# FFN 1's second product in six groups: where the norm vector is scaled, where m4 units are prepared, and when the casting transfers are issued

## The chip, the cores and the metric

The kernel runs on 1 core of one Trainium2 chip. The metric is the device time of one execution in microseconds (us), lower is better. The kernel before takes 1105.27 us, the median of 3 runs (1104.59 to 1105.53).

The engines are named as the profile names them: PE is TensorE (PEld its weight loads), DVE is VectorE, ACT is ScalarE, POOL is GpSimd and SP is SyncE. Each engine works through its own instructions in the order in which the program writes them. SP and POOL also issue DMA transfers, each in its own order.

## The reference

One layer of a hybrid encoder: 512 tokens, 1024 channels, float32. FFN 1, the mixer (a gated linear recurrence and a windowed attention side by side) and FFN 2 follow each other, each with a norm before and after it:

```python
f = swiglu(rms_norm(h, ffn1_pre_g[l]), ffn1_w1[l], ffn1_w3[l], ffn1_w2[l])
h = h + 0.5 * rms_norm(f, ffn1_post_g[l])
u = rms_norm(h, mix_pre_g[l])
q, k, v, xr, xg = jnp.split(u @ w_in[l], splits, axis=-1)
...
def swiglu(x, w1, w3, w2):
    return (jax.nn.silu(x @ w1) * (x @ w3)) @ w2
```

The change concerns the place where the product with `w2` of FFN 1 ends, the two norms behind it are taken (`ffn1_post_g`, then `mix_pre_g`), and the product with `xr` begins. The inner width of the FFN is 2816, that is 22 blocks of 128.

## The kernel before, in words

**Exactness.** Every operand of a product is split in two parts, a rounded one (`hi`) and the remainder (`lo`), and each product is three matmuls (hi x hi, lo x hi, hi x lo). `split2` (L224) is one split: ACT copies to `hi` (L226), DVE subtracts (L227). There are two ways to make `lo` without DVE: ACT copies the negated `hi`, and a DMA transfer that POOL issues adds the source on top. `cast_split` (L168) does so for weights in `BY_CAST`, whose `hi` is written by a transfer that rounds on the way (L147), and `prep` does so for the units in `BY_ADD` (L706 to L709).

**The product with w2 (class `Halves`, L600).** It is done with seven half-sized products instead of eight, in the order m1, m5, m2, m6, m3, m7, m4. Each of the seven goes over G = 6 groups of `w2` blocks (`GS_A`; five groups of two blocks, the last of one), so there are 42 units: 0 to 5 are m1, 24 to 29 m3, 30 to 35 m7, 36 to 41 m4. A unit is 12 matmuls of 128x512, two blocks by two token tiles by three (6 for the last of each six). `prep(n)` (L685) makes the operands of all units below n ready: two weight tiles (`whi`, `wlo`; one in a last unit) and the activations (`uT`, for the units from 36 on a tile `hx` of their own). `step(u)` (L753) calls `prep(u + LEAD)` with `LEAD = 5`, then the unit's hooks, then writes its matmuls. m7 and m4 add up in the same two banks, one for each token tile; between them DVE reads the bank (`out`, L744), so unit 36 has to wait for that.

**The buffers.** All large tiles come from one pool of 42 buffers (`NSLOT`) of 4 KB a partition. A tile that is first written takes the buffer that has been free longest in the order of the program, and its first writer waits until the earlier tile's last readers are done. So a tile that is asked for earlier shifts which buffers the tiles after it get.

**The end of the product (`tok_gemm` with `pre`, L434 to L482).** Steps 0 to 29 are written first, with hooks: after unit 18's preparation the two norm vectors are fetched by POOL (L294), after unit 22's step number ACT scales the second one by a constant (L438, in the order of ACT behind the preparation of unit 26), and at the numbers in `X_AT` = 26, 28, 31, 33 the four casting transfers of `xr` blocks 0 to 3 are issued by POOL. Then `prep(38)` readies units 34 to 37, and norm 0 follows: the norms of token tile 0 (`norms`, L326, with `post_norm`, L297). In the middle of it, behind the row factor (L277) and ahead of the addition to `h` (L322), it calls a function `mid`; before, that is `x_split(0)`, one ACT copy and a POOL transfer. Then units 38 and 39 are readied, `x_split(1)` follows, and steps 30 to 33; units 34 and 35 are written per token tile, with DVE's reading of the bank (L744) behind each, and with the preparation of unit 40 behind the first and unit 41 behind the second. Norm 1 follows with `x_split(2)` as its `mid`, then m4's units for tile 0, the transposes of the normed rows, and so on to norm 3 and the first matmuls with `xr`.

**Line numbers of what the steps touch:** casting transfer L147; negated copy and accumulating transfer of `xr` L172, L174; ACT and DVE part of a split L226, L227; scaling L438; negated copy and transfer in `prep` L707 to L709; matmuls of the units L732 to L734; reading of the bank L744; norm 0: L308 (adding the parts), L310 (squares), L311, L322 (`h`), L334 (squares of `h`), L337, L345 and L346 (normed row); transposes L355.

Of the kernel before, what the change touches and what calls it, by code (L numbers as in the profile page):

```python
# [12 lines left out]
AF = mybir.ActivationFunctionType  # L13
# [38 lines left out]
def hybrid_layer(ctx: ExitStack, tc: tile.TileContext, a: dict, out: bass.AP):  # L52
    nc = tc.nc
    act, dve, pool, pe, sp = nc.scalar, nc.vector, nc.gpsimd, nc.tensor, nc.sync
# [16 lines left out]
    def small(w, name="m", bufs=4):  # L71
        uid[0] += 1
        return sm.tile([P, w], F32, tag=f"sm{w}", name=f"{name}_{uid[0]}", bufs={1: 11, 4: 12}.get(w, bufs))
# [79 lines left out]
    def dma_to(n):  # L153
        while st["dma"] < min(n, len(order)):
            dma_one(st["dma"])
            st["dma"] += 1
# [11 lines left out]
    def cast_split(k):  # L168
        assert k == st["split"]
        dma_to(k + 1)  # L170
        pairs[k] = hi, lo = raws.pop(k), slot([P, D], F32R, name="wlo")
        act.activation(lo, f32(hi), AF.Copy, scale=-1.0)  # L172
        nm, i = order[k]
        pool.dma_start(out=lo, in_=a[nm][i * P : (i + 1) * P, :], accum_op=ALU.add)  # L174
        st["split"] += 1

    def split_to(n):
        while st["split"] < min(n, len(order)) and st["split"] not in paired:
            k = st["split"]
            dma_to(k + 1)  # L180
            r = raws.pop(k)
            if order[k] in BY_DMA:
                nm, i = order[k]
                pairs[k] = split_dma(r, a[nm][i * P : (i + 1) * P, :])
            else:
                hi = slot([P, D], F32R, name="whi")
                lo = slot([P, D], F32R, name="wlo")
                if order[k] in BY_POOL:
                    pool.tensor_copy(hi, r)
                else:  # L190
                    act.activation(hi, r, AF.Copy)
                dve.tensor_tensor(out=lo, in0=r, in1=f32(hi), op=ALU.subtract)
                pairs[k] = (hi, lo)
            st["split"] += 1
# [66 lines left out]
    NEWT = -0.5 * D**0.5  # L261
# [64 lines left out]
    def norms(acc, t, gpost, scale, gpre, spill, eps, mid=None, part=None, ns=(0, 1)):  # L326

        hg = slot([P, D], name="hg")
        junk = slot([P, D], name="junk")
        ss = small(2, "ss")  # L330
        rs = Rstd2()

        def half(n, c):
            act.activation(junk[:, c], h[t][:, c], AF.Square, accum_out=ss[:, n : n + 1])  # L334
            if n:
                rs.first(ss)
                dve.tensor_tensor(out=hg[:, c], in0=h[t][:, c], in1=gpre[:, c], op=ALU.mult)  # L337

        post_norm(acc, t, gpost, scale * NEWT, h[t], half, eps=eps, mid=mid, part=part, ns=ns)
        ht = h[t]  # L340
        if spill:
            sp.dma_start(out=h_scr[t], in_=h.pop(t))
        rs.root(ss)
        r = rs.value()
        dve.scalar_tensor_tensor(out=hg[:, :512], in0=ht[:, :512], scalar=r, in1=gpre[:, :512], op0=ALU.mult, op1=ALU.mult)  # L345
        act.activation(hg[:, 512:], hg[:, 512:], AF.Copy, scale=r)  # L346
        return hg

    def transpose_mm(hg):
        banks = []  # L350
        for half in range(2):
            ps = bank("tr")
            for k in range(4):
                kk = half * 4 + k
                pe.transpose(ps[:, k * P : (k + 1) * P], hg[:, kk * P : (kk + 1) * P], ident)  # L355
            banks.append(ps)
        return banks

    def transpose_out(banks, t, xf=None, parts=(0, 1)):
        c = slice(t * P, (t + 1) * P)  # L360
        for half, ps in enumerate(banks):
            ks = slice(half * 4, half * 4 + 4)
            v = ps.rearrange("p (k c) -> p k c", k=4)
            if 0 in parts:
                act.activation(uT[:, 0, ks, c], v, AF.Copy)
            if 1 in parts:
                dve.tensor_tensor(out=uT[:, 1, ks, c], in0=v, in1=f32(uT[:, 0, ks, c]), op=ALU.subtract)
        if xf:
            transpose_xf(banks, t, xf)

    def transpose_xf(banks, t, xf, halves=(0, 1)):
        for half in halves:
            ps = banks[half]
            v = ps.rearrange("p (k c) -> p k c", k=4)
            act.activation(xf[half, t // 2][:, :, (t % 2) * P : (t % 2 + 1) * P], v, AF.Copy)


    def tok_gemm(nm, xs, n, R, gpost_name, scale, gpre_name, first, x_to=None, xf=None, spill=False, then=None, eps=None, pre=None):
# [34 lines left out]
        g, us, trs = [], {}, {}  # L413
        ep = lambda t: D * EPS if eps is None else eps[:, t : t + 1]

        def vectors():
            g.extend((bcast(gpost_name), bcast(gpre_name)))
            if not pre:
                pool.tensor_scalar(out=g[1], in0=g[1], scalar1=NEWT, scalar2=None, op0=ALU.mult)

        def tails():
            for i, k in enumerate(tail):
                x_to(F + i + 1)
                w[k] = get(nm, k, ahead=max(0, len(tail) - 1 - i), rawahead=0 if pre else 2)
# [6 lines left out]
        def norm(t, mid=None):  # L431
            us[t] = norms(acc[t], t, g[0], scale, g[1], spill, ep(t), mid, pre and pre.part(t), (1, 0) if pre and t > 1 else (0, 1))

        if pre:  # L434
            G = pre.G
            pre.hooks[3 * G].append(vectors)
            pre.hooks[3 * G + 1].append(lambda: act.activation(small(1, "tiny"), veps[:, 0:1], AF.Abs_reciprocal_sqrt))
            pre.hooks[3 * G + 4].append(lambda: act.activation(g[1], g[1], AF.Copy, scale=NEWT))  # L438
            x0 = st["get"] + len(tail)
            for i, u in enumerate(X_AT):  # L440
                pre.hooks[u].append(lambda i=i: dma_to(x0 + i + 1))

            def x_split(i):
                cast_split(x0 + i)

            for u in range(5 * G):
                pre.step(u)
            for t in range(2):
                acc[t] = [pre.bank["bc"][t], pre.bank["bx"][t]]
            pre.prep(5 * G + LEAD + 3)  # L450
            norm(0, lambda: x_split(0))
            pre.prep(7 * G - 2)
            x_split(1)
            for u in range(5 * G, 6 * G - 2):
                pre.step(u)
            for t in range(2):
                for u in range(6 * G - 2, 6 * G):
                    pre.step(u, (t,))
                pre.prep(7 * G - 1 + t)
            for t in range(2, 4):  # L460
                acc[t] = [pre.bank["bu"][t - 2], None]
            pre.hid.eo.clear()
            norm(1, lambda: x_split(2))
            for u in range(6 * G, 7 * G):
                pre.step(u, (0,))
            trs[0] = transpose_mm(us[0])
            transpose_out(trs[0], 0)
            for u in range(6 * G, 6 * G + 2):
                pre.step(u, (1,))
            trs[1] = transpose_mm(us[1])  # L470
            transpose_out(trs[1], 1)
            x_split(3)
            norm(2, lambda: [transpose_xf(trs[0], 0, xf), transpose_xf(trs[1], 1, xf, (0,))])
            transpose_xf(trs[1], 1, xf, (1,))
            for u in range(6 * G + 2, 7 * G):
                pre.step(u, (1,))
            pre.bank.clear()
        else:
            tails()
            vectors()  # L480
            split_to(st["get"] + len(first))
            dma_to(st["split"] + 2)  # L482
            for t in range(NT):
                for n_ in range(2):
                    classical(t, n_)
                if t == NT - 1:
                    break
                if t >= 1:
                    trs[t - 1] = transpose_mm(us[t - 1])
                if t == NT - 2:  # L490
                    transpose_out(trs[t - 1], t - 1)
                norm(t)
                if t == 1:
                    transpose_out(trs[t - 1], t - 1, xf)

        t = NT - 1
# [103 lines left out]
    class Halves:  # L600
# [84 lines left out]
        def prep(self, n, load=True):  # L685

            G = self.G
            while self.ready < min(n, self.cap):
# [16 lines left out]
                src = self.again.pop(i) if m == "m3" else self.raw[b, i]  # L705
                if (self.nm, m, i) in BY_ADD:  # L706
                    act.activation(hi, src, AF.Copy)  # L707
# [483 lines left out]
    for k in range(KT):  # L1191
        if k % 2 == 0:
            split_first(0, k // 2)
        g = vec[:, V_G1 + k : V_G1 + k + 1]
# [662 lines left out]
BY_POOL = {("wg", i) for i in range(2, 8)} | {("wk", 0), ("wk", 1)}  # L1857

BY_CAST = {("xr", i) for i in range(4)}
BY_ADD = {("w2a", "m7", 3)}  # L1860

TAIL_A = ()
LEAD = 5
# [1 line left out]
LOAD_A, LOAD_B = (0, 3, 5, 5), (0, 4, 5, 6)  # L1865
GS_A = (4, 6), (8, 10), (12, 14), (16, 18), (0, 20), (2,)
MARKS_A = (), (), (27, 31, 33, 34)
X_AT = (26, 28, 31, 33)

TAIL_B = ()  # L1870
GS_B = (0, 2), (4, 6), (8, 10), (12, 14), (16, 18), (20,)
# [64 lines left out]
```

## Time and profile before

| | |
|---|---|
| runs before (3) | 1104.59 to 1105.53 us, median 1105.27 |
| the profiled execution's own time | 1104.66 us |
| its span (first to last instruction) | 1102.7 us |
| PE busy | 1089.6 us (99%) |
| PEld busy | 986.2 us (89%) |
| DVE busy | 936.6 us (85%) |
| ACT busy | 708.4 us (64%) |
| POOL busy | 426.7 us (39%) |
| mean granted TensorE clock | 0.996 |
| DMA traffic | 158.04 MB, mean 143 GB/s |

The profile is one execution of the program, taken by the hardware profiler. A timeline row gives the start and the duration in us from the span's start, engine, line, operation, the tile that is written and those read, the shape, and in brackets how long the engine was idle just before it and what released it. "x2" means two merged instructions. A row of the view of waits reads: who waited, for whom, us in total, how often, the longest. A row of the view of windows reads: stretch, its length, then for PE, PEld, DVE, ACT and POOL the busy time and the number of instructions, the granted TensorE clock (1.00 is full speed), the DMA share and GB/s. A row of DMA groups reads: tile written and source, issuing engine, number, KB each, median us from issue to landing. Matmuls are pipelined, so their durations overlap; the distance of their starts is their rate.

### The profile page before, as it was taken

How to read it: one execution, taken by the hardware profiler on the slowest of the kernel's cores; microseconds unless marked ns; L12 is line 12 of the kernel's file. 1: busy time of each engine (PE TensorE's matmuls, PEld its weight loads, DVE VectorE, ACT ScalarE, POOL GpSimd, SP SyncE). 2: the span in 40 equal slices, each digit the busy share in tenths (PEclk: the TensorE clock that was granted, in tenths of full speed). 3: DMA queues.
4: the chain of work that ended last, by engine and by line, in shares of the span. 5: the costliest groups of instructions: out<-in, count | busy, mean ns of one | idle time of the engine just before them, and what ended most of it. 6: DMA issues, size and time to landing. Idle time of an engine off the chain costs nothing.

```text
span 1102.7 us, 18128 instructions
## 1 busy us (share of the span) xinstructions
PE 1089.6 (99%) x6850; PEld 986.2 (89%) x6850; DVE 936.6 (85%) x1346; ACT 708.4 (64%) x1240; POOL 426.7 (39%) x356
## 2 busy tenths in 40 slices
PE   9999999999989999999999999999999999999997
PEld 7899999998869877899888888888999999998885
DVE  5998999999898998888678867767889989889996
ACT  7756555598777778756656564456555555578872
POOL 0144833232211523233557574010877656633200
PEclk9999999999999999999999999999999999999999
DMA  9325663399858653146222245352323323449923
GB/s 327 132 80 143 145 134 115 111 198 214 237 151 234 186 130 108 40 158 246 75 78 95 95 156 210 134 186 80 137 77 116 101 92 106 147 102 242 213 73 132
DMA packets 54761, 158.04 MB, mean 143 GB/s; under 512 B 5633, under 2 KB 7553, under 8 KB 54673
## 3 DMA queue, kind: packets, MB, share of 16 engines
q1 hardware_dynamic: 40560, 122.75, 32.6%
q0 software_dynamic: 13824, 33.60, 16.2%
q8 instruction: 54, 0.88, 0.3%
q10 hardware_dynamic: 288, 0.52, 0.2%
q14 instruction: 35, 0.28, 0.1%
HBM read 140.61 MB, written 13.62 MB: 140 GB/s over the span
## 4 chain that ended last, share of the span: by engine, by line
PE 98%; DVE 1%; issue 0%; DMA 0%; ACT 0%; DVEq 0%; ACTq 0%
PE c L843 13%; PE c L845 13%; PE c L844 13%; PE f L237 10%; PE f L238 9%; PE f L239 9%; PE hw L732 6%; PE hw L733 6%; PE hw L734 6%; PE acc L257 1%; PE acc L255 1%; PE acc L256 1%; PE pt L1696 1%; PE s L1660 1%; PE s L1659 1%; PE tr L355 1%
## 5 line engine op out<-in xcount | busy, mean ns | idle before, releaser
L844 PE MATMUL c<-uT,wlo 128*128 128x256 f32 x516 | 146.0, 283 | 0.0
L845 PE MATMUL c<-uT,whi 128*128 128x256 f32 x516 | 146.0, 283 | 0.0
L843 PE MATMUL c<-uT,whi 128*128 128x256 f32 x516 | 146.0, 283 | 0.0
L843 PE MATMUL c<-Xh,whi 128*128 128x256 f32 x504 | 142.7, 283 | 0.0
L844 PE MATMUL c<-Xh,wlo 128*128 128x256 f32 x504 | 142.6, 283 | 0.0
L237 PE MATMUL f<-uT,whi 128*128 128x512 f32 (+1 forms) x380 | 138.6, 365 | 0.0
L238 PE MATMUL f<-uT,wlo 128*128 128x512 f32 (+1 forms) x380 | 136.9, 360 | 0.0
L239 PE MATMUL f<-uT,whi 128*128 128x512 f32 (+1 forms) x380 | 136.9, 360 | 0.0
L845 PE MATMUL c<-Xl,whi 128*128 128x256 f32 x456 | 129.1, 283 | 0.0
L227 DVE TENSOR_TENSOR wlo<-S,whi 128x1024 fp32r<-128x1024 f32 x86 | 117.8, 1370 | 6.4 <-ACT whi L226 3.2
L226 ACT ACTIVATE whi<-S 128x1024 fp32r<-128x1024 f32 x86 | 88.4, 1054 | 37.7 <-DVE S L892 36.5
L844 PEld LDWEIGHTS c<-uT,wlo 128*128 128x128 f32 x516 | 99.0, 192 | 0.2
L843 PEld LDWEIGHTS c<-uT,whi 128*128 128x128 f32 x516 | 99.0, 192 | 0.2
L845 PEld LDWEIGHTS c<-uT,whi 128*128 128x128 f32 x516 | 99.0, 192 | 0.0
L843 PEld LDWEIGHTS c<-Xh,whi 128*128 128x128 f32 x504 | 96.8, 192 | 0.3 <-issue 0.3
L844 PEld LDWEIGHTS c<-Xh,wlo 128*128 128x128 f32 x504 | 96.8, 192 | 0.0
L732 PE MATMUL hw<-whi,uT 128*128 128x512 f32 x240 | 93.4, 389 | 0.0
L734 PE MATMUL hw<-whi,uT 128*128 128x512 f32 x240 | 93.4, 389 | 0.0
L845 PEld LDWEIGHTS c<-Xl,whi 128*128 128x128 f32 x456 | 87.5, 192 | 0.0
L733 PE MATMUL hw<-wlo,uT 128*128 128x512 f32 x216 | 84.0, 389 | 0.0
L237 PEld LDWEIGHTS f<-uT,whi 128*128 128x128 f32 x380 | 71.7, 189 | 12.1 <-issue 1.4
L239 PEld LDWEIGHTS f<-uT,whi 128*128 128x128 f32 x380 | 71.7, 189 | 11.0
(422 smaller groups left out, 3220.2 us busy)
## 6 DMA issues: line engine op xcount, KB each, us to landing
raw_w1b<-in_w1b_dram SPq DMA_DIRECT2D x22, 512.0 KB, 4.3
raw_w3b<-in_w3b_dram SPq DMA_DIRECT2D x22, 512.0 KB, 4.3
raw_w3a<-in_w3a_dram SPq DMA_DIRECT2D x21, 512.0 KB, 4.7
raw_w1a<-in_w1a_dram SPq DMA_DIRECT2D x20, 512.0 KB, 4.3
raw_wg<-in_wg_dram SPq DMA_DIRECT2D x16, 512.0 KB, 3.8
raw_w2a<-in_w2a_dram SPq DMA_DIRECT2D x15, 512.0 KB, 7.2
raw_w2a<-in_w2a_dram POOLq DMA_DIRECT2D x15, 512.0 KB, 9.8
raw_w2b<-in_w2b_dram SPq DMA_DIRECT2D x15, 512.0 KB, 6.4
```

Of the source, the lines that this page charges most:

```text
L226: act.activation(hi, src, AF.Copy)
L227: dve.tensor_tensor(out=lo, in0=src, in1=f32(hi), op=ALU.subtract)
L237: pe.matmul(ps[:, c0:c1], wh[:, s], h_, start=k == 0 and c0 == 0, stop=False, skip_group_check=True)
L238: pe.matmul(ps[:, c0:c1], wl[:, s], h_, start=False, stop=False, skip_group_check=True)
L239: pe.matmul(ps[:, c0:c1], wh[:, s], l_, start=False, stop=k == KT - 1, skip_group_check=True)
L255: pe.matmul(acc[n], x[:, 0, c], wh[:, s], start=first, stop=False, skip_group_check=skip)
L732: pe.matmul(ps, xs[:, 0, j, c], hi[:, j, :], start=start and j == 0, stop=False, skip_group_check=True)
L733: pe.matmul(ps, xs[:, 0, j, c], lo[:, j, :], start=False, stop=False, skip_group_check=True)
L734: pe.matmul(ps, xs[:, 1, j, c], hi[:, j, :], start=False, stop=i == self.G - 1, skip_group_check=True)
L843: pe.matmul(ps, wh[:, s], xh, start=first, stop=False, skip_group_check=True)
L844: pe.matmul(ps, wl[:, s], xh, start=False, stop=False, skip_group_check=True)
L845: pe.matmul(ps, wh[:, s], xl, start=False, stop=k == 3, skip_group_check=True)
```

## The change

Five edits, all for FFN 1's `w2`:

- ACT scales the second norm vector right ahead of norm 0, behind the preparation of units 34 to 37, and no longer in the hook at 22.
- The `mid` of norm 0 is the preparation of unit 38; only unit 39 is readied after the norm, and `x_split(0)` comes behind that.
- `x_split(1)` moves from ahead of step 30 to behind unit 35's first half and the preparation of unit 40.
- Unit 36 (m4, group 0) joins `BY_ADD`: its `lo` part is made by ACT and a transfer instead of by DVE.
- The four casting transfers are issued at units 25, 26, 27 and 28.

```diff
             pre.hooks[3 * G + 1].append(lambda: act.activation(small(1, "tiny"), veps[:, 0:1], AF.Abs_reciprocal_sqrt))
-            pre.hooks[3 * G + 4].append(lambda: act.activation(g[1], g[1], AF.Copy, scale=NEWT))
...
             pre.prep(5 * G + LEAD + 3)
-            norm(0, lambda: x_split(0))
-            pre.prep(7 * G - 2)
-            x_split(1)
+            act.activation(g[1], g[1], AF.Copy, scale=NEWT)
+            norm(0, lambda: pre.prep(6 * G + 3))
+            pre.prep(6 * G + 4)
+            x_split(0)
             for u in range(5 * G, 6 * G - 2):
                 pre.step(u)
             for t in range(2):
                 for u in range(6 * G - 2, 6 * G):
                     pre.step(u, (t,))
                 pre.prep(7 * G - 1 + t)
+                if t == 0:
+                    x_split(1)
...
-BY_ADD = {("w2a", "m7", 3)}
+BY_ADD = {("w2a", "m7", 3), ("w2a", "m4", 0)}
...
-X_AT = (26, 28, 31, 33)
+X_AT = (25, 26, 27, 28)
```

## The prediction

> **What bounds the kernel now.** The profiled execution took 1104.66 us, its span is 1102.7 us, and TensorE is busy for 99% of it. So I read first, in the view of waits, what TensorE waits for. It lists one behind the start of the kernel:
>
> ```profile
> PE hw L732 <- DVE hc L744: 4.3, 1, 4.3
> ```
>
> TensorE's timeline around it, start and duration first; the 17 steps from 317.77 to 321.62 are the steady rate, 0.227 us a matmul:
>
> ```profile
> 317.77 0.39 PE L732 MATMUL hw<-whi,uT 128*128 128x512 f32 x1
> ...
> 321.62 0.39 PE L734 MATMUL hw<-whi,uT 128*128 128x512 f32 x1
> 326.28 0.47 PE L732 MATMUL hw<-whi,hx 128*128 128x512 f32 x1 [4.27 <-DVE hc L744]
> ...
> 330.23 0.39 PE L733 MATMUL hw<-wlo,hx 128*128 128x512 f32 x1
> ```
>
> Unit 35 ends at 321.62 + 0.227 = 321.85, unit 36 (m4's first) starts at 326.28: 4.43 us lost. Then ten matmuls take 330.23 - 326.28 = 3.95 us instead of 2.27: 1.68 more. The row of those 5 us shows the granted clock (the number behind the POOL column):
>
> ```profile
> 326.00:331.00 5.00, 4.72 (x14) 3.77 (x15) 4.90 (x10) 1.89 (x5) 1.13 (x3) 0.66 1.02 333
> ```
>
> So 6.1 us are to be had here at most. Counting back from 317.77 (unit 34) at 12 matmuls a unit, 6 for unit 29: units 33, 32 start at 315.05, 312.33; units 27, 26, 25, 24 at 300.09, 297.36, 294.64, 291.92.
>
> Unit 36 adds to the bank that L744 reads, and L744 for the first token tile stands in VectorE's queue behind all of norm 0 and the splits of units 38 and 39. Unit 35 was done with that tile at 317.77 + 9 x 0.227 = 319.8. VectorE is late. Why, its timeline shows:
>
> ```profile
> 295.17 1.23 DVE L227 TENSOR_TENSOR wlo<-raw_w2a,whi 128x1024 fp32r<-128x1024 f32 x1 [3.87 <-ACT whi L226]
> ...
> 311.29 1.22 DVE L227 TENSOR_TENSOR wlo<-raw_w2a,whi 128x1024 fp32r<-128x1024 f32 x1
> 312.42 0.68 DVE L227 TENSOR_TENSOR hx<-hEO,hx 128x512 fp32r<-128x512 f32 x1
> 313.03 0.68 DVE L308 TENSOR_TENSOR hc<-hw,hc 128x512 f32<-128x512 f32 x1
> ...
> 317.05 1.42 DVE L322 SCALAR_TENSOR_TENSOR h<-fg,r,h 128x512 f32<-128x512 f32 x2
> ...
> 325.45 0.68 DVE L744 TENSOR_TENSOR hc<-hw,hc 128x512 f32<-128x512 f32 x1
> ```
>
> Norm 0 starts at 313.03 (L308), its row factor is there at 317.05 (L322), L744 comes at 325.45. ScalarE's timeline has the cause of the 3.87 us and the pace of the preparations:
>
> ```profile
> 287.82 1.06 ACT L226 ACTIVATE whi<-raw_w2a 128x1024 fp32r<-128x1024 f32 x1 [1.14 <-PE hw L733]
> 288.79 0.61 ACT L226 ACTIVATE uT<-hEO 128x512 fp32r<-128x512 f32 x1
> 293.13 1.06 ACT L438 ACTIVATE bc_mix_pre_g<-bc_mix_pre_g 128x1024 f32<-128x1024 f32 x1 [3.73 <-DMA bc_mix_pre_g<-in_mix_pre_g_dram]
> 294.10 1.04 ACT L226 ACTIVATE whi<-raw_w2a 128x1024 fp32r<-128x1024 f32 x1
> ...
> 303.22 1.05 ACT L707 ACTIVATE whi<-raw_w2a 128x1024 fp32r<-128x1024 f32 x1
> ...
> 305.79 1.04 ACT L226 ACTIVATE whi<-raw_w2a 128x1024 fp32r<-128x1024 f32 x1
> ...
> 307.26 0.62 ACT L226 ACTIVATE whi<-raw_w2a 128x512 fp32r<-128x512 f32 x1
> ...
> 316.36 1.05 ACT L172 ACTIVATE wlo<-whi 128x1024 fp32r<-128x1024 f32 x1
> ...
> 320.26 0.72 ACT L346 ACTIVATE hg<-hg,r 128x512 f32<-128x512 f32 x1 [0.72 <-DVE r L277]
> 320.89 1.04 ACT L226 ACTIVATE whi<-raw_w2a 128x1024 fp32r<-128x1024 f32 x1
> ```
>
> A unit costs ScalarE 307.26 - 305.79 = 1.47 us, the half as wide unit 35 a little over half of it (I take 0.83), a unit in BY_ADD (unit 33) 305.79 - 303.22 = 2.57. The first row shows the other rule of this stage: a preparation also waits for a buffer that TensorE frees.
>
> **The change, part by part.**
>
> *Scaling moved.* ScalarE no longer stands from 289.4 to 293.13 for the vector, nor scales it there: unit 27 can start at 289.3 instead of 294.10, 4.8 us earlier. The vector has then been there for long, and the 0.97 us of scaling lie behind unit 37 while ScalarE waits for L308: nothing, unless ScalarE is later than VectorE there.
>
> *Casting transfers earlier.* They take their buffers at once. Before, POOL shows them waiting for these:
>
> ```profile
> 290.99 0.55 POOL L147 DMA_DIRECT2D whi<-in_xr_dram  x1 [9.01 <-DVE wlo L227]
> 300.55 0.53 POOL L147 DMA_DIRECT2D whi<-in_xr_dram  x1 [9.01 <-PE hw L734]
> ...
> 325.70 1.43 POOL L147 DMA_DIRECT2D whi<-in_xr_dram  x2
> ```
>
> By the program's rule a new tile takes the buffer that has been free longest, so two transfers pulled ahead of units 32 and 33 push every later tile of the stage two buffers on, and units 30 and 31 one. Following that order: unit 31's first tile now takes a buffer that unit 25's matmuls free (297.36), unit 32's one that unit 26 frees (300.09), and unit 33's second one unit 27 frees (302.8); unit 33's first stays free of TensorE. **This eats most of the 4.8 us.** ScalarE then runs: unit 32 at 300.09, unit 33 at 301.56, its negated copy at 302.8, unit 34 at 304.3, unit 35 at 305.8, unit 36 at 306.6.
>
> *Unit 36 by accumulating transfer.* VectorE saves one 1.14 us subtraction (311.29 to 312.42 is one), ScalarE pays 2.57 - 1.47 = 1.10: unit 37 starts at 309.2. It is now ScalarE that sets the pace, so this edit costs here. VectorE: subtraction 1.07 us after 309.2 (as 294.10 to 295.17), then 1.13 and 0.61: norm 0 starts at 312.0 instead of 313.03, **1.0 us earlier**. The transfer itself issues near 309; unit 36 is due after 325. It may wait to land as unit 33's did or longer, at no cost:
>
> ```profile
> whi<-in_xr_dram POOLq DMA_DIRECT2D x4, 512.0 KB, 7.6
> ...
> wlo<-raw_w2a POOLq DMA_DIRECT2D x1, 512.0 KB, 4.4
> ```
>
> Unit 33's own transfer now issues near 304 behind four casting ones of 7.6 us (median) and is due at 315.05. That leaves 11 us; even both rows in sequence (12.0) would cost about 1 us, in a stall that lies ahead of the larger one and so is absorbed by it. I take nothing.
>
> *Unit 38 inside norm 0.* After the row factor ScalarE prepares unit 38 (from 315.3 where it had the negated copy of 316.36). VectorE's two splits end 1.07 + 1.13 + 0.61 = 2.8 us after that, at 318.1; L322 would have come at 316.0, so the rest of norm 0 is 2.1 us longer. L322 to L346 took 320.26 - 317.05 = 3.21: L346 at 321.3. Then unit 39: ScalarE 0.63 later, VectorE 1.07 after that, 1.13 + 0.61: **L744 at 324.75** instead of 325.45. From L308 to L744 it was 325.45 - 313.03 = 12.4 us and is now 12.75: the unit that no longer stands behind the norm stands inside it, and VectorE waits for ScalarE once more. So this edit costs 0.3, and -1.0 + 0.3 = -0.7 us.
>
> *x_split moved.* The negated copies of xr0 and xr1 come after unit 39 and after unit 40, behind what L744 for the first tile needs. Their accumulating transfers then issue near 325 and 328, and xr's matmuls stand behind all 66 of m4 (15.0 us from 325.6 on): nothing. In norm 1 a wait goes:
>
> ```profile
> 334.52 1.06 ACT L172 ACTIVATE wlo<-whi 128x1024 fp32r<-128x1024 f32 x1 [1.82 <-DMA whi<-in_xr_dram]
> ```
>
> TensorE waited for nothing behind this, so its going gains nothing by itself; it keeps norm 1 from being late when TensorE is earlier.
>
> **Sum.** L744 0.7 us earlier, TensorE 0.83 us behind it (326.28 - 325.45): unit 36 at 325.6, gap 3.7 us. Whether the slow clock after the gap goes is not shown: before has one gap, 4.27 us idle and followed by it. The bounds are 0 and 1.68; 3.7 is nearest to 4.27, so I take 0. 1104.66 - 0.7 = **1104.0 us**. TensorE waits nowhere after it, so the gain lasts to the end. The median of the runs, 1105.27, lies 0.6 above the profiled execution; so the forecast's own range is 1103.5 to 1104.8.
>
> [...]
>
> **Rivals.**
>
> *The clock stays up* in the shorter gap: 1104.66 - 0.7 - 1.68 = 1102.3. For it: before does not show at which length between nothing and 4.27 us the clock begins to fall; against it: the gap has nearly its old length.
>
> *The cover is complete.* If the buffers came out so that no preparation waits for units 25 to 27, norm 0 would gain 4.8 - 1.1 = 3.7 us; with unit 38's 0.3 that it costs, L744 comes 3.3 us earlier, the gap is 1.1, the clock stays: 1104.66 - 3.3 - 1.7 = 1099.7. For it: the row at 294.10 onwards has no wait for TensorE; against it: the row at 287.82.
>
> *It doesn't do what it says.* If unit 33's first tile takes a buffer of unit 27, ScalarE starts it at 302.8 instead of 301.56, norm 0 starts at 313.1, and unit 38's 0.3 us inside the norm remain: 1104.66 + 0.4 = 1105.0.
>
> *Slower: unit 38 waits for a buffer in the middle of norm 0.* Two buffers on, its tiles may be freed by later matmuls than I count. From 316.0 on each us comes on top of before. Unit 33's end (317.77) gives +1.8, 1106.4; the first half of unit 34 in its second tile, which ends at 317.77 + 15 x 0.227 = 321.17, moves unit 38 by 5.9 us and unit 36 to 331.5: 1104.66 + 5.2 = 1109.9. For it: the stage lives at the limit of the pool; against it: norm 0 had its own tiles without such a wait.
>
> **How the numbers follow.** Forecast 0.32, clock up 0.20, cover complete 0.20, doesn't do it 0.10, slower 0.18. Range 1099.7 to 1106.0: from the complete cover to just above the third rival with the 0.6 us between execution and median; only the slow case is left out. 0.2% (about what a measurement tells from no change) is 2.2 us: clock up and complete cover are faster (0.40), forecast and third rival within (0.42), slower 0.18.
>
> **What would show it.** ScalarE's wait of 3.73 us gone and unit 27 near 289; waits for TensorE at units 31 and 32 near 297.4 and 300.1; L308 at 312.0; L744 at 324.75; a wait of TensorE of about 3.6 us on L744; the granted clock behind it low or not; no wait of ScalarE at the third negated copy. I am wrong if the wait on L744 falls under 2 us (buffers), or if ScalarE waits inside norm 0.

## The result and the profile after

The changed kernel takes 1103.22 us (median of 20 runs, 1101.65 to 1104.92). The kernel before took 1105.26 us beside it (median of 20, 1104.54 to 1107.96). The ratio is 0.998, with a 95% interval of 0.9974 to 0.9987: 2.0 us faster. The profiled execution took 1103.08 us, with a span of 1101.3 us (before 1104.66 and 1102.7). Lines behind the moved code have numbers two higher than before: L746 is L744 of before, L734 to L736 are L732 to L734, L709 to L711 are L707 to L709, and the scaling is L450.

The view of waits still lists one wait of TensorE behind the start, a little shorter:

```profile
PE hw L734 <- DVE hc L746: 3.5, 1, 3.5
```

TensorE's timeline of the changed kernel has unit 35's last matmul, unit 36's first and unit 36's eleventh:

```profile
321.37 0.39 PE L736 MATMUL hw<-whi,uT 128*128 128x512 f32 x1
325.30 0.47 PE L734 MATMUL hw<-whi,hx 128*128 128x512 f32 x1 [3.54 <-DVE hc L746]
...
329.25 0.39 PE L735 MATMUL hw<-wlo,hx 128*128 128x512 f32 x1
```

The gap is 325.30 - 321.37 - 0.23 = 3.70 us, where it was 4.43. The ten matmuls behind it take 3.95 us again. The view of windows has the reason, the granted clock (the third number from the end) of the same five microseconds as before:

```profile
326.00:331.00 5.00, 5.00 (x17) 3.93 (x16) 4.80 (x10) 2.32 (x6) 0.86 (x1) 0.68 1.06 243
```

This execution stands 0.25 us earlier than the one before when it reaches the stage (321.37 against 321.62), so 0.25 us has to be added to a time of it before it is held against the prediction's. ScalarE's timeline: unit 27, units 31 and 32, the negated copy of unit 33, unit 36 with its negated copy, unit 37, the scaling, unit 38 inside norm 0, the third negated copy of `xr`:

```profile
289.06 1.04 ACT L226 ACTIVATE whi<-raw_w2a 128x1024 fp32r<-128x1024 f32 x1
...
297.09 1.07 ACT L226 ACTIVATE whi<-raw_w2a 128x1024 fp32r<-128x1024 f32 x1 [0.85 <-PE hw L735]
...
300.04 1.06 ACT L226 ACTIVATE whi<-raw_w2a 128x1024 fp32r<-128x1024 f32 x1 [1.37 <-PE hw L736]
...
302.60 1.06 ACT L710 ACTIVATE wlo<-whi 128x1024 fp32r<-128x1024 f32 x1
...
306.39 1.04 ACT L709 ACTIVATE whi<-raw_w2a 128x1024 fp32r<-128x1024 f32 x1
307.46 1.06 ACT L710 ACTIVATE wlo<-whi 128x1024 fp32r<-128x1024 f32 x1
...
308.95 1.04 ACT L226 ACTIVATE whi<-raw_w2a 128x1024 fp32r<-128x1024 f32 x1
...
310.42 1.05 ACT L450 ACTIVATE bc_mix_pre_g<-bc_mix_pre_g 128x1024 f32<-128x1024 f32 x1
...
315.04 1.04 ACT L226 ACTIVATE whi<-raw_w2a 128x1024 fp32r<-128x1024 f32 x1
...
331.76 1.04 ACT L172 ACTIVATE wlo<-whi 128x1024 fp32r<-128x1024 f32 x1
```

Unit 27 starts 4.8 us sooner after the scaling has gone (289.06 + 0.25 against 294.10). Units 31 and 32 then wait for TensorE, which they did not do before: that is where the gain goes. VectorE's timeline: the start of norm 0, unit 38 inside it, the new `h`, unit 39, the reading of the bank:

```profile
311.77 0.68 DVE L308 TENSOR_TENSOR hc<-hw,hc 128x512 f32<-128x512 f32 x1
...
316.12 1.23 DVE L227 TENSOR_TENSOR wlo<-raw_w2a,whi 128x1024 fp32r<-128x1024 f32 x1 [0.42 <-ACT whi L226]
...
317.86 1.41 DVE L322 SCALAR_TENSOR_TENSOR h<-fg,r,h 128x512 f32<-128x512 f32 x2
...
322.72 1.23 DVE L227 TENSOR_TENSOR wlo<-raw_w2a,whi 128x1024 fp32r<-128x1024 f32 x1 [1.01 <-ACT whi L226]
...
324.47 0.68 DVE L746 TENSOR_TENSOR hc<-hw,hc 128x512 f32<-128x512 f32 x1
```

POOL's timeline has the casting transfers issued in pairs, each pair held until TensorE frees buffers, and all four well ahead of norm 0:

```profile
294.63 1.08 POOL L147 DMA_DIRECT2D whi<-in_xr_dram  x2 [12.91 <-PE hw L736]
300.07 1.07 POOL L147 DMA_DIRECT2D whi<-in_xr_dram  x2 [4.35 <-PE hw L736]
```

TensorE's last matmul of the whole program starts at 1094.81 us before and 1093.78 us after: 0.25 of the 1.03 us is the start, 0.73 the gap. Between that matmul and the end of the span lie 7.9 us before and 7.5 us after.

### The profile page after: what moved, and what is told of

Read it like the earlier page. It is cut to its first block, busy times and chain, and to the rows that moved or that the text cites. A ratio compares the mean times of both kernels' runs of the same rounds, so it can differ in the third digit from the quotient of the medians.

```text
span 1101.3 us, 18142 instructions
## 1 busy us (share of the span) xinstructions
PE 1089.4 (99%) x6850; PEld 986.4 (90%) x6850; DVE 934.8 (85%) x1345; ACT 709.9 (64%) x1241; POOL 427.8 (39%) x357
## 4 chain that ended last, share of the span: by engine, by line
PE 97%; ACT 1%; DVE 1%; issue 1%; DMA 0%; DVEq 0%; SPq 0%; ACTq 0%
PE c L845 13%; PE c L846 13%; PE c L847 13%; PE f L237 10%; PE f L238 9%; PE f L239 9%; PE hw L734 6%; PE hw L736 6%; PE hw L735 6%; PE acc L256 1%; PE acc L257 1%; PE acc L255 1%; PE pt L1698 1%; PE s L1662 1%; PE s L1661 1%; PE tr L355 1%
## 5 line engine op out<-in xcount | busy, mean ns | idle before, releaser
L736 PE MATMUL hw<-whi,uT 128*128 128x512 f32 x240 | 93.5, 390 | 0.0
L734 PE MATMUL hw<-whi,uT 128*128 128x512 f32 x240 | 93.5, 390 | 0.0
```

The lines of the kernel that those rows point to most:

```text
L734: pe.matmul(ps, xs[:, 0, j, c], hi[:, j, :], start=start and j == 0, stop=False, skip_group_check=True)
L736: pe.matmul(ps, xs[:, 1, j, c], hi[:, j, :], start=False, stop=i == self.G - 1, skip_group_check=True)
```

## The experiments

Four theories are named in the expectations. **A** is the prediction's: the scaling's new place would give almost the whole wait back, and the early casting transfers, by pushing later tiles on to buffers that TensorE frees late, eat most of it; the transfer of unit 36 and unit 38 inside the norm cost a little more. **B** says that the early transfers and the other edits brought the gain. The other two are about the part of the 2.0 us that a gap shorter by 0.7 us does not explain: **C** says that it is the clock behind the gap, **E** that it is the landing of the third casting transfer, for which norm 1 waits. In e3 and e4 a rival to C is called D.

### e1: the scaling alone

The kernel before with one edit:

```diff
-            pre.hooks[3 * G + 4].append(lambda: act.activation(g[1], g[1], AF.Copy, scale=NEWT))
...
             pre.prep(5 * G + LEAD + 3)
+            act.activation(g[1], g[1], AF.Copy, scale=NEWT)
             norm(0, lambda: x_split(0))
```

> Of the five edits only the scaling is moved, all else as before. Theory A (the buffers pushed on by the early casting transfers ate the gain): without them units 31 and 32 start on ACT near 296 and 297.6 without waiting for TensorE, norm 0 starts near 309 instead of 311.8 in the changed kernel, the bank is read near 321.3, TensorE waits some 0.5 us there instead of 3.5, the granted clock stays at 1.0 behind it, and the wait for the third casting transfer in norm 1 comes back and costs about 1 us at the transposes: some 1099.4 us, 5.9 less than before and 3.8 less than the changed kernel. Theory B (it is the early casting transfers and unit 36's transfer that brought the gain, the units wait for TensorE's buffers anyway): norm 0 starts at 311.8 or later, 1103 to 1105 us.

Measured: 1099.9 us (5 runs, 1099.73 to 1101.56), ratio 0.9956 (0.9944 to 0.9969). One edit out of five is worth 5.4 us, 3.3 us more than all five together. Its waits of TensorE behind the first product's start:

```profile
PE tr L355 <- DVE hg L345: 1.1, 1, 1.1
PE hw L732 <- DVE hc L744: 0.3, 1, 0.3
```

The wait on the reading of the bank has gone from 4.27 to 0.33 us, and no slow clock follows (1.00 from 322 to 332 us). The expectation, which had about 1 us at the transposes in it, is 0.5 us too low; where that 0.5 us lies is not shown. The first line is the wait that it expected. TensorE now gets to the transposes of tile 1 while norm 1 still waits for the third casting transfer, as ScalarE's timeline of this kernel shows; before, the long gap hid that wait:

```profile
331.08 1.06 ACT L172 ACTIVATE wlo<-whi 128x1024 fp32r<-128x1024 f32 x1 [2.01 <-DMA whi<-in_xr_dram]
```

### e2: the changed kernel with the casting transfers late again

```diff
-X_AT = (25, 26, 27, 28)
+X_AT = (26, 28, 31, 33)
```

> The changed kernel with the casting transfers put back to units 26, 28, 31 and 33. Theory A: units 31 and 32 no longer wait for TensorE, norm 0 starts near 309.3, TensorE waits some 1.3 us for the bank, the clock stays up, and about 1 us comes back at norm 1's transposes: some 1100.3 us, 2.9 less than the changed kernel. Theory B: the gain of the changed kernel goes with the transfers, 1104 to 1105 us.

Measured: 1100.54 us (5 runs, 1100.19 to 1100.96), ratio 0.9959 (0.9945 to 0.9972). Units 31 and 32, whose rows follow from ScalarE's timeline, come one behind the other without a wait, 1.0 and 2.4 us sooner than in the changed kernel when counted from unit 35 (whose last matmul starts at 321.56 here):

```profile
296.32 1.05 ACT L226 ACTIVATE whi<-raw_w2a 128x1024 fp32r<-128x1024 f32 x1
...
297.79 1.05 ACT L226 ACTIVATE whi<-raw_w2a 128x1024 fp32r<-128x1024 f32 x1
```

The view of waits gives TensorE's wait on the reading of the bank:

```profile
PE hw L734 <- DVE hc L746: 1.2, 1, 1.2
...
PE tr L355 <- DVE hg L345: 0.3, 1, 0.3
```

So the numbers in `X_AT` cost the changed kernel 2.4 us of wait and the slow clock: 2.7 us in the medians, 3.4 us between the two profiled executions from unit 35 to the last matmul. A is borne out from both sides (e1 adds the scaling, e2 takes the early transfers away), and B falls.

### e5: the changed kernel without unit 36's transfer

```diff
-BY_ADD = {("w2a", "m7", 3), ("w2a", "m4", 0)}
+BY_ADD = {("w2a", "m7", 3)}
```

> The changed kernel with one edit undone: unit 36's low part is made by VectorE again. Theory A (after the change ScalarE sets the pace of units 30 to 37 through the buffers, so unit 36's extra negated copy of 1.1 us costs): unit 37 starts about 1.1 us earlier on ScalarE, VectorE's first step of norm 0 comes 0.4 us earlier (near 311.3, frames apart by start noise), TensorE's wait on the reading of the bank falls from 3.5 to about 3.1 us: 1102.7 us, ratio to before 0.9977. Theory B (this edit brought part of the gain, VectorE is the pace): the subtraction of 1.14 us comes back in VectorE's queue, norm 0 starts 0.7 to 1.1 us later, wait 4.3 us: 1104.0 us or more.

Measured: 1101.4 us (6 runs, 1101.06 to 1104.05), ratio 0.9968 (0.9955 to 0.998). Unit 36 on TensorE's timeline:

```profile
325.15 0.77 PE L734 MATMUL hw<-whi,hx 128*128 128x512 f32 x1 [3.08 <-DVE hc L746]
```

Norm 0's start on VectorE's timeline:

```profile
311.63 0.68 DVE L308 TENSOR_TENSOR hc<-hw,hc 128x512 f32<-128x512 f32 x1
```

Unit 35's last matmul starts at 321.68 here, so norm 0 begins 0.45 us earlier than in the changed kernel, against the same point, and the gap is 3.24 us and not 3.70. A's 0.4 us is what the edit costs; that ScalarE and not VectorE sets the pace is shown. The time fell by more, and the next sections say why.

### e6: units 38 and 39 both behind norm 0

```diff
-            norm(0, lambda: pre.prep(6 * G + 3))
+            norm(0)
```

> The changed kernel with one edit undone: nothing is prepared inside norm 0, units 38 and 39 are both readied behind it. Theory A (the prediction's term: inside the norm VectorE waits for ScalarE once more, which costs 0.3 us): the reading of the bank comes 0.3 us earlier, TensorE's wait about 3.2 us, 1102.9 us, ratio 0.998. Rival: inside the norm unit 38 fills time in which VectorE waits for ScalarE's row factor anyway, so taking it out makes the reading of the bank later by up to 1 us: wait 4.5 us, 1104.2 us.

Measured: 1102.91 us (11 runs, 1102.61 to 1104.3), ratio 0.9982 (0.9973 to 0.9991). The reading of the bank on VectorE's timeline:

```profile
324.01 0.68 DVE L746 TENSOR_TENSOR hc<-hw,hc 128x512 f32<-128x512 f32 x1
```

Unit 36's first matmul and a later one on TensorE's timeline:

```profile
324.85 0.47 PE L734 MATMUL hw<-whi,hx 128*128 128x512 f32 x1 [3.15 <-DVE hc L746]
...
326.33 0.63 PE L734 MATMUL hw<-whi,hx 128*128 128x512 f32 x1
```

The gap is 3.31 us: the unit inside the norm costs 0.39 us, as A said (0.3). The second line matters below. Matmuls of 0.63 us, at a granted clock of 0.50, begin some 1.4 us after TensorE has resumed.

### e7: the early casting transfers alone

The kernel before with the diff of e2 the other way round.

> The kernel before with one edit alone: the casting transfers at 25, 26, 27 and 28. Theory A: the preparations run later than the buffers' releases already, so nothing changes at norm 0, the wait on the reading of the bank stays at 4.3 us and the slow clock behind it; in norm 1 the wait of ScalarE for the third casting transfer (1.8 us) is gone. Then the two explanations of the rest of the gain part. C (the rest is the clock, which comes in several sizes from run to run): median 1105.2 us, same spread as before (1103.9 to 1105.9). E (the rest is the late landing of that transfer, which in many runs of the kernel before makes TensorE wait in norm 1): median near 1104.3, the upper group of the runs gone.

Measured: 1104.06 us (11 runs, 1103.65 to 1105.0), ratio 0.9991 (0.9982 to 1.0). Alone the edit is worth 1.0 us, with an interval that reaches to nothing. Its one wait of TensorE behind the start:

```profile
PE hw L732 <- DVE hc L744: 4.2, 1, 4.2
```

Nothing moves at norm 0, as A says (the gap is 4.32 us), and ScalarE's wait in norm 1 is gone. The time is the one that E named, but nine of the eleven runs have a mean granted clock of 0.996 to 0.997, and only two 0.995, where more than half of the runs of before have 0.995. So most of the runs moved with the clock, for which C gives no reason here; neither theory predicted this. Another 0.4 us is not clock: the nine have a median of 1103.97 us where runs of before with that clock have 1104.37, and behind the last matmul e7 takes 7.5 us where before takes 7.9.

### e3, e4 and e9: matmuls that fill the gap

All three have extra matmuls outside the computation, into a bank that nobody reads, so that TensorE is busy while it waits: 26 in the changed kernel (e3), 32 in the kernel before (e4), 32 with the early casting transfers alone (e9).

```diff
+    def fill(n):
+        ps = bank("w")
+        for _ in range(n):
+            pe.matmul(ps[:, :256], uT[:, 0, 0, :P], uT[:, 0, 0, :256], start=True, stop=True)
...
             norm(1, lambda: x_split(2))
+            fill(32)
```

> The changed kernel with 26 matmuls of 128x256 (about 3.1 us) into a bank that nobody reads, in TensorE's order right ahead of unit 36, so that they fill most of its 3.7 us gap; they add work outside the computation and take no wait away. [...] Rival D (the half speed is no matter of the gap): 1103.2 us as without them.

> The kernel before with 32 such matmuls (about 3.8 us) right ahead of unit 36, in its 4.4 us gap. Theory C: all runs near 1102.5 us (1101.7 and the 0.7 us that its gap is longer), that is 2.8 us less than before's median, so that half speed cost the kernel before 2.8 us in the middle run and the changed one 1.5, and 1.3 of the 2.0 us gained are clock. Rival D2 (half speed costs both kernels the 1.7 us of their profiles): 1103.6 us. Rival D (no matter of the gap): 1105.3 us.

> The kernel before with the early casting transfers alone and the 32 filler matmuls in the gap (extra work whose result nobody reads). With the fillers alone the slow stretch went, and TensorE then waited 0.9 us in norm 1, behind ScalarE's wait for the third casting transfer. C (clock and transfer are two costs in a row, the slow clock hid the transfer): wait for the reading of the bank as before, no slow stretch, no wait in norm 1: 0.9 us less than the fillers alone at least, 1103.2 us or less, and the runs in one group. Rival (the 0.9 us is norm 1 itself, late by VectorE's own queue): wait of about 0.9 us in norm 1 stays, 1104.1 us or more.

Measured: e3 1102.47 us (10 runs), ratio 0.9977 (0.9967 to 0.9986); e4 1104.41 us (11 runs, 1103.74 to 1105.31), ratio 0.9993 (0.9984 to 1.0002); e9 1102.64 us (11 runs, 1102.37 to 1103.7), ratio 0.998 (0.9971 to 0.9989). From unit 36 to the first transpose TensorE takes 7.60, 7.59 and 7.61 us in them, at a granted clock of 1.00, against 9.19 before and 9.21 after: a slow stretch is worth 1.6 us. C's times were missed all the same, by 0.8 us in e3 (1101.7 us, that of the changed kernel's two quickest runs) and by 1.9 us in e4. In e4, TensorE's timeline shows where part of it went (the filler's lines move the numbers behind them: L360 is L355 of before, and L738 and L750 below are L732 and L744):

```profile
338.21 1.09 PE L360 MATMUL tr<-ident,hg 128*128 128x128 f32 x8 [0.90 <-DVE hg L345]
```

ScalarE's timeline shows who is late:

```profile
334.16 1.06 ACT L172 ACTIVATE wlo<-whi 128x1024 fp32r<-128x1024 f32 x1 [1.80 <-DMA whi<-in_xr_dram]
```

It is the wait of e1 again. With the early transfers (e9) it is gone, TensorE's list of waits is only this, and the median is 1.8 us lower than e4's (the profiled spans differ by 0.9 us, 1101.1 against 1102.0):

```profile
PE w L1159 <- POOL warm L1156: 1.1, 1, 1.1
PE hw L738 <- DVE hc L750: 0.3, 1, 0.3
PE f L1209 <- ACT uT L1202: 0.2, 1, 0.2
```

So the early transfers do have a worth, about 1 us, but only where TensorE comes to norm 1 early enough; the landing might also explain the spread of e4's runs at one clock, which is not shown. In e3 about 0.7 us of the 1.6 is lost between 530 and 717 us, 0.3 of it in a wait that the changed kernel does not have:

```profile
PE f L237 <- DVE o L1735: 0.3, 1, 0.3
```

Why it does is open; e9, with such a filler too, shows no such wait.

### e10, e11, e12: the clock behind the gap, in further profiles

The same kernels once more, for further profiles: the kernel before (e10, e12) and that of e5 (e11).

> The kernel before once more, for a second profile. Its runs have a mean granted clock of 0.996 to 0.997 at 1103.9 to 1104.7 us or of 0.995 at 1105.0 to 1105.9 us; the profiled one was of the first kind, with 3.4 us at clock 0.50. C: if this one is of the second kind, its profile shows two such stretches in a row (6.8 us at 0.50), of which the first begins inside the wait, and unit 36 to the first transpose takes 10.3 us and not 9.2. E: it shows the same 3.4 us and instead a wait of TensorE of about 1 us in norm 1.

> The changed kernel without unit 36's transfer once more, for a second profile. [...] Rival (a gap of this length always costs one slow stretch, and the runs differ elsewhere): 9.2 us or more again.

> The kernel before a third time, for a profile of its longer runs (mean clock 0.995, 1105.0 to 1105.9 us), which more than half of its runs are. C: such a profile shows two stretches at clock 0.50 in a row, 6.8 us together, the first beginning some 0.5 to 3 us inside the wait, unit 36 to the first transpose about 10.3 us. E: one stretch and a wait of TensorE in norm 1. If this execution is of the shorter kind (0.996 to 0.997) it shows one stretch of 3.4 us again and decides nothing.

Measured: 1104.15, 1104.49 and 1104.37 us, one run each, with mean clocks of 0.996, 0.995 and 0.997. The window from 322 to 332 us of four profiles tells how much slow clock lies in it, by the granted clock again, the third number from the end. The changed kernel:

```profile
322.00:332.00 10.00, 6.70 (x22) 5.38 (x23) 8.90 (x15) 7.29 (x14) 1.73 (x2) 0.83 1.04 292
```

The scaling alone (e1):

```profile
322.00:332.00 10.00, 9.67 (x47) 7.85 (x46) 8.71 (x16) 4.21 (x10) 1.52 (x3) 1.00 0.95 307
```

e5:

```profile
322.00:332.00 10.00, 6.92 (x19) 5.44 (x19) 9.07 (x16) 7.35 (x14) 1.73 (x2) 0.66 1.03 279
```

e11, the same kernel as e5:

```profile
322.00:332.00 10.00, 6.92 (x19) 5.21 (x18) 8.86 (x15) 7.35 (x14) 1.73 (x2) 0.66 1.03 285
```

In these profiles' rows of 0.25 us the clock is 1.00 or 0.50, but for the rows in which it changes. So 0.83 over 10 us is 3.4 us at half, and 0.66 is 6.8 us: one stretch, or two in a row. From the fall to the return these rows give 3.41 to 3.42 us for one and 6.83 us for two (e5, e11). By the mean clock of e5's six runs, 0.998 in four, none was held the most likely for e11; it has two. In the mean over a whole run of 1102 us one stretch is 3.4 x 0.5 / 1102 = 0.0015. All 14 profiles agree with that ladder: mean 0.998 to 0.999 without a stretch (e1, e2, e3, e4, e8, e9), 0.996 to 0.997 with one (before, changed, e6, e7, e10, e12), 0.995 with two (e5, e11). Read by it, which is an estimate, the mean clock of a run without a profile tells its stretches:

| kernel (gap) | no stretch | one | two |
|---|---|---|---|
| before (4.43 us), 57 runs beside the experiments | 0 | 25, median 1104.37 | 32, median 1105.46 |
| changed (3.70 us), 20 runs | 2, near 1101.7 | 15, median 1103.22 | 3, 1104.4 to 1104.9 |
| e5 (3.24 us), 6 runs | 4, near 1101.3 | 1, 1102.5 | 1, 1104.05 |
| e6 (3.31 us), 11 runs | 0 | 8 | 3 |
| e7 (4.32 us), 11 runs | 0 | 9, median 1103.97 | 2 |

Neither of the two further profiles of before was one of its 32 longer runs, so two stretches behind its gap are read from the mean clock and were not seen directly. That the longer runs have a lower mean clock speaks against E, by which they would only wait longer. e10 and e12 decide nothing there, but e12 shows how late a stretch can begin. TensorE resumes at 326.17, and the clock falls only behind 327 (the granted clock of these two microseconds):

```profile
326.00:327.00 1.00, 0.83 (x4) 0.73 (x5) 1.00 (x2) 1.00 (x3) 1.00 (x2) 1.00 0.99 406
327.00:328.00 1.00, 1.00 (x5) 0.76 (x3) 1.00 (x3) 0.05 (x1) 0.01 (x1) 0.59 1.08 442
```

The same kernel's first profile and e10, each in the microsecond in which the clock falls:

```profile
326.00:327.00 1.00, 0.72 (x3) 0.60 (x4) 1.00 (x2) 1.00 (x3) 1.00 (x3) 0.87 1.06 434
```

```profile
325.00:326.00 1.00, 0.00 (x0) 0.00 (x0) 1.00 (x3) 1.00 (x2) 0.91 (x2) 0.85 1.06 434
```

So in three executions of one kernel the clock falls at 326.74 (the first), 325.71 (e10) and 327.18 us (e12), while TensorE resumes at 326.28, 326.21 and 326.17 us: the gap keeps its place and the fall does not. What sets the place of the fall is not shown. The eight profiles with a stretch have so much of TensorE's gap, in us, in the 3.41 us ahead of the fall (the length of one stretch) and behind the fall:

| profile | ahead of the fall | behind the fall | stretches |
|---|---|---|---|
| changed | 2.90 | 0 | one |
| before | 2.95 | 0 | one |
| e6 | 1.99 | 0 | one |
| e7 | 2.63 | 0 | one |
| e12 | 2.40 | 0 | one |
| e10 | 3.41 | 0.50 | one |
| e5 | 2.22 | 1.02 | two |
| e11 | 2.47 | 0.77 | two |

The two profiles with a second stretch are those with the most of the gap behind the fall, 0.77 and 1.02 us; whether that is the cause is not shown.

### e8: a version that beats both

The scaling's new place, and the last two casting transfers right ahead of norm 0, so that units 30 to 37 take their buffers first (line numbers behind the moved code are one higher than before):

```diff
-            pre.hooks[3 * G + 4].append(lambda: act.activation(g[1], g[1], AF.Copy, scale=NEWT))
...
             pre.prep(5 * G + LEAD + 3)
+            act.activation(g[1], g[1], AF.Copy, scale=NEWT)
+            dma_to(x0 + 4)
             norm(0, lambda: x_split(0))
...
-X_AT = (26, 28, 31, 33)
+X_AT = (26, 28)
```

> The kernel before with the scaling right ahead of norm 0, and the last two casting transfers issued there too instead of at 31 and 33: the other edits are left out. Theory A: units 30 to 37 take the buffers they take with the scaling alone or better, so the wait on the reading of the bank is under 1 us, the clock stays up, and the third transfer lands ahead of its use in norm 1, so TensorE's wait of 1.1 us there goes too: 1098.8 us, ratio 0.994. Rival B (the early issue is what counts, order of buffers is unimportant): as the scaling alone, 1099.9 us, or worse where the issue ahead of norm 0 takes buffers from units 38 and 39 (a wait of ScalarE for TensorE inside or behind norm 0, 1101 us or more).

Measured: 1098.48 us (5 runs, 1098.44 to 1098.9), ratio 0.994 (0.9925 to 0.9954): 6.6 us faster than before, 4.7 us faster than the changed kernel. TensorE's whole list of waits:

```profile
PE w L1154 <- POOL warm L1151: 1.1, 1, 1.1
PE hw L733 <- DVE hc L745: 0.3, 1, 0.3
```

The order of buffers for units 30 to 37 stays, the third transfer is there for norm 1, and the clock stays up (1.00 from 322 to 332 us). A expected 1098.8.

## Why the prediction was right, and where it was short

The forecast was 1104.0 us and the median is 1103.22, inside the whole range and 0.3 us under the forecast's own (1103.5 to 1104.8). The mechanism holds, with its sizes; one term, the clock, was taken from a single profile. Of the 2.04 us by which the median fell, only 0.73 are the shorter gap that the sum forecast.

*Scaling moved.* Right: the wait of 3.73 us is gone, and unit 27 starts 4.8 us earlier. e1 shows what this is worth without the rest: 5.4 us.

*Casting transfers push the buffers on.* Right, to 0.2 us: units 31 and 32 were forecast for 297.36 and 300.09 and start at 297.34 and 300.29 in before's time. The negated copy of unit 33 was forecast for 302.8 and starts at 302.85. e2 shows that this order of buffers alone costs 2.4 us of the gap. The prediction's rival of the complete cover (1099.7) is the kernel without it: e2, the changed kernel with the transfers late, gave 1100.54, and e1 1099.9. (Its sum has a slip: 3.7 less 0.3 is 3.4 and not 3.3; in e2 the gap is 3.1 us shorter than before.)

*Unit 36's transfer costs.* Right: the prediction said that it costs and gave no number for it alone; e5 shows 0.46 us. The saving of 1.14 us on VectorE bought nothing, because ScalarE had become the one that is late.

*Unit 38 inside norm 0 costs 0.3.* Right: 0.39 in e6. The norm ran as forecast (L322 at 318.1, measured 317.86 + 0.25), without a wait for a buffer, so the slower rival fell; no profile shows anything of it.

*`x_split` moved, for nothing.* The wait at the third negated copy is gone, but that was the transfers' doing: e7 has the copies in their old places and does not wait either. That the early landing "keeps norm 1 from being late when TensorE is earlier" is shown by e1, e4 and e9: about 1 us, and worth nothing in the changed kernel.

*The sum.* -0.7 us for the reading of the bank; measured, the gap is 0.73 us shorter.

*The clock, taken as unchanged.* This is the step that was mis-sized. In the two profiled executions it is unchanged: one stretch of 3.4 us in each. But the prediction read the 0.6 us between before's profiled execution and its median as something to add to the range, and it was a second stretch: 32 of 57 runs of before have two, and 3 of 20 of the changed kernel. Between runs with one stretch each, the medians differ by 1104.37 - 1103.22 = 1.15 us: 0.73 of the gap, and about 0.4 at the end of the span, where before and e4 take 7.9 us behind the last matmul and all the other kernels 7.5 to 7.6. That 0.4 us repeats in each of the three profiles of before and is not explained. The remaining 0.9 of the 2.04 us is the median run's second stretch. The rival "the clock stays up" (1102.3) also happened, in two of the 20 runs.

Why one and the same gap is followed by one stretch in one run and by two in another is not shown: in the section on e12 the gap of before keeps its place and the fall moves by 1.47 us. So the share of runs with two stretches, 32 of 57 for before, 3 of 20 for the changed kernel and 2 of 11 for e7, stays open, and so does why the changed kernel and e5 have runs without one where before, e6 and e7 have none.

## What to carry to other kernels

Where tiles come from one pool in the order in which they are asked for, a transfer that is issued early can be paid for by the tiles behind it (e2), though not where these are late for another reason (e7): follow which buffers those get before calling an early issue free, and ask for it behind the tiles that are late. When a stall falls, look for the wait that it hid, and move that one's cause without touching the order that the first gain rests on (e8). Where the clock falls behind a stall, as it did here with gaps of 3.24 to 4.43 us, read the mean clock of many runs and not only the one profile, for the same kernel can stand on different steps of it.

## What the runs showed of the hardware

Gaps of 3.24 us (e5, e11) and 3.31 us (e6) go with a granted clock of 0.50 in their profiles, one of 1.33 us (e2) does not (1.00 from 322 to 332 us); by their mean clock, four of the six runs of e5 had none. The fall does not come at the gap's end. It came 1.0 us ahead of TensorE's return in e5, and about 1.0 us behind it in e12 and 1.4 us in e6. The clock stays at 0.50 for 3.4 us, or for 6.8 us in e5 and e11, where the fall came 0.8 to 1.0 us ahead of the return; in e10 it came 0.5 us ahead, and there was one stretch. In e6 the 3.4 us ahead of the fall at 326.27 hold 1.4 us of matmuls. The prediction took the slow clock as unchanged behind a gap of 3.7 us; by their mean clock, 18 of the 20 runs of the changed kernel have a stretch. The casting transfers land sooner with their earlier issue, 5.0 us in the median where it was 7.6, by the row of DMA groups of the changed kernel:

```profile
whi<-in_xr_dram POOLq DMA_DIRECT2D x4, 512.0 KB, 5.0
```
